# Held operands of the last down phase: own tiles, two transfers, earlier splits

## The chip, the cores and the metric

The kernel runs on one core of a Trainium2 chip. The metric is the device time of one execution in microseconds (us), as the median of several runs. The profile is one execution, taken by the hardware profiler; it names the engines PE (TensorE matmul), PEld (its weight loads), DVE (VectorE), ACT (ScalarE), POOL (GpSimd) and SP (SyncE, which issues nearly all transfers here).

## The reference

The kernel computes one decoder block in float32: attention and pooling heads, then a SwiGLU feed-forward layer, both between RMS norms with scale, shift and gate from a conditioning vector. The change lies in the last line of the feed-forward part:

```python
h = rmsnorm(x, g_ffn_pre[l]) * (1.0 + scale_f) + shift_f
f = (jax.nn.silu(h @ w_gate[l]) * (h @ w_up[l])) @ w_down[l]
x = x + gate_f * rmsnorm(f, g_ffn_post[l])
```

There are 2048 tokens, a model width of 1024 and a feed-forward width of 2816, which is 22 chunks of 128.

## The kernel before

**The number format.** Every float32 operand of a matmul is split in two: a rounded copy on ACT (line 59, the "high" part, type fp32r) and the remainder on DVE (line 60, the "low" part). A product takes three matmuls: high with high, low with high, high with low (lines 69 to 71).

**The down stage.** The tokens are worked on in two halves of 1024 (`sb` 0 and 1). The product with `w_down` is done in Strassen's manner (seven products of quarter matrices for eight): in each half `down` runs seven phases, p1, p2, p6, p7, p5, p4, p3, in that order. A phase has 11 steps (`HF`), one for each chunk of 128 rows of the inner dimension. A step needs a piece `g` of the gated activations and a piece `w` of the weights, 128x512 each; it makes 12 matmuls, three into each of four PSUM banks (`HK` row blocks).

**How a step gets its operands.** `load_g` brings `g` in groups of four chunks (1 MB, two buffers in turn), `load_w` brings `w` one chunk at a time (256 KB, four buffers); both are asked for five steps ahead. `split_gw` splits both, 2 casts on ACT and 2 subtractions on DVE, into pairs from a ring of five and one more (`operand`). The order on PE, ACT, DVE and POOL is the order of the program text; the order of SP's queue is left to the compiler's scheduler. In the loop over steps, for step n first everything registered ahead for n is written out, then the matmuls, then the splits as far as the window of steps holds no more than six pairs (`PAIRS`, two per step: the split of step n+2), then the "takes": the operations that read a finished phase's banks, one or a few steps later.

**The last phase.** In p3 of the second half the last four chunks (7 to 10, `HELD`) are held back: their steps issue no matmuls, and their split pairs go to tiles of their own in the pool `dn1`, not to the ring. After them come four tail steps, one for each row block, that run the 12 held matmuls of that row block, so that the rows are finished one after the other.

**What is around it.** While p3 runs, the takes of p4 finish rows 4 to 7 of the half. For a row i: an addition from PSUM on DVE (line 1363, `y_v`), its square on ACT with the sum (line 1366), a multiply by the gate on POOL (line 1367), the norm (lines 1384 and 1385 on DVE, the power on POOL, line 1386), and the end in two halves: a multiply-add on DVE (line 1394), and a scale on ACT (line 1396) with an addition on POOL (line 1397). Each half is stored by SP (line 1398). The takes of p3, behind the tail steps, do the same for rows 0 to 3 (`y_u`); the very last row's multiply by the gate and both its ends are on DVE. The takes of p5, while p4 runs, add from PSUM, square and multiply by the gate (`c_4` to `c_7`).

Of the kernel before, what the change touches and what calls it, by code (L numbers as in the profile page):

```python
# [9 lines left out]
F32 = mybir.dt.float32  # L10
F32R = mybir.dt.float32r
# [6 lines left out]
P = 128  # L18
# [10 lines left out]
TB = 512  # L29
# [6 lines left out]
PRB = 6  # L36
FT = {"sr": 4, "p1": 1, "u2": 2, "u3": 2, "u4": 1, "cu": 2, "s": 6, "gs": 3, "tr": 4, "gf": 1}
PAIRS, HELD = 6, 4
RB = PAIRS - 1
LOAD_AT = (-20, -8)  # L40
SPLIT_AT = ((-14, -11, -8, -5), (-8, -6, -4, -2))
# [3 lines left out]
def block_kernel(ctx, tc, x, c, w_cond, b_cond, g_mix_pre, g_mix_post, w_in, w_pool,  # L45
                 pool_scale, w_out, g_ffn_pre, g_ffn_post, w_gate, w_up, w_down, out):
    nc = tc.nc
# [6 lines left out]
    def raw(ap):  # L54
        return ap.bitcast(F32)

    def split(hi, lo, src, low=nc.vector):

        nc.scalar.copy(hi, src)  # L59
        low.tensor_tensor(lo, src, raw(hi), ALU.subtract)  # L60
# [12 lines left out]
    def open_pool(stack, name, bufs=1, side=None):  # L73
        kw = {"side": side} if side else {}
        return stack.enter_context(tc.tile_pool(name=name, bufs=bufs, reuse_waits="tile", **kw))
# [4 lines left out]
    def dt(name, shape):  # L80
        return dram.tile(shape, F32, tag=name, name=name)
# [8 lines left out]
    ga = [{n: dt(f"ga{sb}{n}", [P, NF // 2, TB]) for n in ("a11", "a12", "s1", "s2", "s3", "s4", "a22")} for sb in range(2)]  # L90
# [15 lines left out]
    def ft(tag, name, shape=(P, TB)):  # L106
        return fx.tile(list(shape), F32, tag=tag, bufs=FT[tag], name=name)
# [893 lines left out]

    ring = open_pool(ctx, "ring", bufs=RB)
    SBT = S // 2
    NTS = SBT // P
    HF = NF // 2
# [3 lines left out]
    def operand(name):  # L1009
        used[0] += 1  # L1010
        pool = fx if fx is not None and used[0] % (RB + 1) == 0 else ring
        return [pool.tile([P, TB], F32R, tag=f"w{n}", bufs=1 if pool is fx else RB, name=f"{name}_{n}") for n in "hl"]

# [267 lines left out]
    def down(sb, dn):  # L1281
# [12 lines left out]
        def add_block(ps, i, j, g, w):  # L1294
            cols = slice(i * P, (i + 1) * P)
            mm3(ps, [((g[0][:, cols], g[1][:, cols]), w)], first=j == 0, last=j == HF - 1)

        def phase(n, a, b, parts, held=0):

            if b[0] == "b":  # L1300
                src = wd_rows[b[1] == "2"][:, :, (b[2] == "2") * TB:][:, :, 0:TB]
            else:
                src = td[b]
            ph = {}
            QF = 3 if n == "p1" else 4

            def chunk(j):
                name = f"{sb}{n}_{j}"

                def load_g():  # L1310
                    m = min(QF, HF - j)
                    t = (ring, fx)[len(quads) % 2].tile([P, 4, TB], F32, tag="w32", bufs=1, name=f"g{name}")
                    quads.append(t)
                    ph["gq", j // QF] = t
                    nc.sync.dma_start(t[:, 0:m], ga[sb][a][:, j:j + m, :])

                def load_w():
                    ph["w", j] = t = ft("tr", f"w{name}")
                    nc.sync.dma_start(t, src[:, j, :])

                def split_gw():
                    pairs = []
                    for kind, s in (("g", ph["gq", j // QF][:, j % QF, :]), ("w", ph["w", j])):
                        if j >= HF - held:
                            pair = [dn().tile([P, TB], F32R, tag=f"{kind}k{l}", bufs=held, name=f"{kind}{name}{l}") for l in "hl"]
                        else:
                            pair = operand(f"{kind}{name}")
                        split(*pair, s)
                        pairs.append(pair)
                    ph[j] = pairs  # L1330

                def mm():
                    if j == 0:
                        ph["ps"] = [f_ps(f"dn{sb}{n}_{i}") for i in range(HK)]
                    for i in range(HK):
                        add_block(ph["ps"][i], i, j, *ph[j])

                s = Step(2, split_gw, mm)
                if j % QF == 0:
                    s.ahead.append((5, load_g))  # L1340
                s.ahead.append((5, load_w))
                if j == HF - 1:
                    s.take = [(1 + m + (i if n == "p3" and m < 2 else 2 * i), lambda i=i, f=f: f(i, ph["ps"][i]))
                              for i in range(HK) for m, f in enumerate(parts)]
                if held and j >= HF - held:
                    s.mm = lambda: None
                    s.take = []
                return s

            r = [chunk(j) for j in range(HF)]  # L1350
            if held:
                def tail(i):
                    def mm():
                        for j in range(HF - held, HF):
                            add_block(ph["ps"][i], i, j, *ph[j])
                    after = [(i, f) for f in parts[:2]] + ([(i - 1, parts[3])] if i else []) + [(i, parts[2])]
                    after += [(i, parts[3])] * (i == HK - 1)
                    return Step(0, lambda: None, mm, [(1, lambda i=i, f=f: f(i, ph["ps"][i])) for i, f in after])
                r += [tail(i) for i in range(HK)]
            return r  # L1360
# [91 lines left out]
        r = []  # L1452
        for n, a, b, parts in (
                ("p1", "a11", "b11", [p1]),
                ("p2", "a12", "b21", [p2, lambda i, ps: first_half_done(i, ps)]),
                ("p6", "s2", "t2", [p6]),
                ("p7", "s3", "t3", [p7]),
                ("p5", "s1", "t1", [p6, p5, p5_done]),
                ("p4", "a22", "t4", [p4, lambda i, ps: half_done(st["v"][i], HK + i, 0, ps), lambda i, ps: norm(HK + i), p4_end]),
                ("p3", "s4", "b22", [p6, p3_done, lambda i, ps: norm(i), p3_end])):  # L1460
            r += phase(n, a, b, parts, HELD if sb and n == "p3" else 0)
# [117 lines left out]
```

## Time and profile before

| what | value |
|---|---|
| runs | median 2336.19 us of 3 (2331.99 to 2337.07) |
| profiled execution | 2336.15 us |
| its span, first to last instruction | 2334.4 us |
| granted PE clock, mean | 0.99 |
| stretch 2229 to 2281 us: PE, DVE, ACT, POOL busy | 52.00, 30.85, 24.05, 5.18 us |
| 2281 to 2305 us | 24.00, 18.08, 13.32, 8.57 us |
| 2305 to 2326 us | 14.12, 14.74, 6.69, 13.83 us |
| 2326 to 2334 us | 0.00, 4.06, 1.24, 2.37 us |

The profile's lines give a start or a count, durations, the engine, the source line, and the output and input tiles by their names; a bracket names the idle time before the operation and what ended it. In a line of a timeline the first number is the start in us from the start of the span, the second the duration in us. Durations overlap a little (a new operation begins up to 0.08 us before the shown end of the one before). A stretch's line has the busy time of each engine with its count, then the granted clock of PE, the busy share of the DMA engines and their GB/s. In the chain of waits each piece is the work, or "issue" where no work is shown, that the next one waited for. A step of the down stage takes about 2.75 us, and p3 begins near 2285.5 us, p4 near 2255.2, p2 near 2134.

### The profile page before, as it was taken

Reading aid. Unit: us, or ns where it says so; the run is one execution under the profiler, and the core shown is the slowest. Engines: PE = TensorE matmul, PEld = TensorE weight load, DVE = VectorE, ACT = ScalarE, POOL = GpSimd, SP = SyncE. Lnnn points to the kernel's source line nnn. Section 1 sums busy time; section 2 is a strip of 40 time slices with the busy share of each in tenths; the row PEclk is TensorE's granted clock in tenths of the full one; section 3 lists DMA queues with packets and bytes.
Section 4 is the critical chain, followed back from the end, with each engine's and each line's share of the span. In section 5 each row is a group of like instructions: output and inputs, shape, how many; then the busy total and the mean of one; then the engine's idle time right before and its main releaser. Section 6 shows DMA issues by size and latency. Waiting matters only on the chain.

```text
span 2334.4 us, 33386 instructions
## 1 busy us (share of the span) xinstructions
PE 2268.4 (97%) x10717; PEld 1863.7 (80%) x10717; DVE 1633.2 (70%) x2222; ACT 1165.1 (50%) x2411; POOL 1317.9 (56%) x1621
## 2 busy tenths in 40 slices
PE   6999999999999999999999999999999999999997
PEld 4778888888888778787888888788888888888885
DVE  6774559999999966756666665886766555565556
ACT  4323658889988854444323232554533323234444
POOL 4542347787778854555787878430486665641004
PEclk9999999999999999999999999999999999999998
DMA  8785764343435636665545455876753333327664
GB/s 288 250 291 194 275 189 118 100 109 89 129 100 147 174 100 203 212 204 179 168 157 158 156 160 183 267 248 212 249 184 112 109 118 91 113 86 281 194 196 145
DMA packets 307116, 405.17 MB, mean 174 GB/s; under 512 B 19254, under 2 KB 179578, under 8 KB 303868
## 3 DMA queue, kind: packets, MB, share of 16 engines
q1 hardware_dynamic: 302620, 400.68, 53.8%
q10 hardware_dynamic: 4320, 2.36, 0.4%
q8 instruction: 84, 1.38, 0.3%
q14 instruction: 92, 0.75, 0.1%
HBM read 274.51 MB, written 128.45 MB: 173 GB/s over the span
## 4 chain that ended last, share of the span: by engine, by line
PE 81%; DVE 5%; POOL 4%; DMA 4%; issue 3%; ACT 2%; SPq 1%; POOLq 0%; DVEq 0%; ACTq 0%
PE wt L838 4%; PE t_u L71 3%; PE t_u L70 3%; PE t_u L69 3%; PE t_g L70 3%; PE t_g L69 3%; PE t_g L71 3%; PE dn0p L70 3%; PE dn0p L71 3%; PE dn0p L69 3%; PE dn1p L69 3%; PE dn1p L70 3%; PE dn1p L71 3%; PE av L853 3%; PE av L854 2%
## 5 line engine op out<-in xcount | busy, mean ns | idle before, releaser
L827 POOL TENSOR_TENSOR w<-sg,pr 128x512 f32<-128x512 f32 (+2 forms) x320 | 307.8, 962 | 41.6 <-DVE pr L821 22.2
L1186 POOL TENSOR_TENSOR s<-s,cu 128x512 f32<-128x512 f32 x88 | 133.8, 1528 | 239.0 <-DVE cu L1185 138.5
L821 DVE TENSOR_TENSOR_SCAN pr<-pr,carry,idle 128x512 f32<-128x512 f32 x192 | 244.3, 1272 | 0.0
L808 ACT ACTIVATE sg<-z 128x512 f32<-128x512 f32 (+2 forms) x320 | 180.8, 565 | 56.2 <-PE z L806 25.8
L60 DVE TENSOR_TENSOR wtl<-wt,wth 128x512 fp32r<-128x512 f32 (+1 forms) x320 | 189.9, 594 | 26.8 <-ACT wth L59 25.5
L59 ACT CAST wth<-wt 128x512 fp32r<-128x512 f32 (+1 forms) x320 | 179.5, 562 | 12.8 <-PE wt L838 12.8
L810 ACT ACTIVATE pr<-z 128x512 f32<-128x512 f32 (+2 forms) x320 | 179.9, 562 | 0.0
L838 PE MATMUL wt<-ident,w 128*128 128x128 f32 x1088 | 173.7, 274 | 3.7 <-POOL w L827 1.9
L60 DVE TENSOR_TENSOR u_s_l<-u_s,u_s_h 128x512 fp32r<-128x512 f32 x66 | 66.6, 1010 | 151.5 <-ACT u_s_h L59 151.4
L838 PEld LDWEIGHTS wt<-ident,w 128*128 128x128 f32 x1088 | 129.3, 141 | 31.0 <-POOL w L827 2.6
L1176 ACT ACTIVATE s<-s 128x512 f32<-128x512 f32 x88 | 55.7, 633 | 193.3 <-DVE s L1175 193.3
L853 PE MATMUL av<-wth,vt 128*128 128x512 f32 (+1 forms) x320 | 129.2, 404 | 5.9 <-ACT o L858 5.8
L70 PE MATMUL dn0p<-w0p_l,g0p_h 128*128 128x512 f32 x308 | 121.2, 394 | 2.6 <-DVE w0p_l L60 2.6
L60 DVE TENSOR_TENSOR u_a_l<-u,u_a_h 128x512 fp32r<-128x512 f32 x66 | 79.1, 1200 | 61.9 <-ACT u_a_h L59 61.9
L69 PE MATMUL dn0p<-w0p_h,g0p_h 128*128 128x512 f32 x308 | 120.5, 391 | 0.0
L854 PE MATMUL av<-wtl,vt 128*128 128x512 f32 (+1 forms) x320 | 118.8, 371 | 1.7 <-DVE wtl L60 1.3
L71 PE MATMUL dn0p<-w0p_h,g0p_l 128*128 128x512 f32 x308 | 120.4, 391 | 0.0
L803 PE MATMUL z<-kt,qt 128*128 128x512 f32 (+2 forms) x320 | 117.9, 369 | 1.9 <-ACT pr L810 1.3
L59 ACT CAST g_s_h<-g_s 128x512 fp32r<-128x512 f32 x66 | 39.5, 620 | 159.6 <-POOL g_s L1118 83.4
L804 PE MATMUL z<-kt,qt 128*128 128x512 f32 (+2 forms) x320 | 117.0, 366 | 0.0
L59 ACT CAST u_s_h<-u_s 128x512 fp32r<-128x512 f32 x66 | 38.6, 614 | 151.9 <-POOL u_s L1118 151.9
L70 PE MATMUL dn1p<-w1p_l,g1p_h 128*128 128x512 f32 x292 | 114.4, 392 | 0.0
(657 smaller groups left out, 7302.7 us busy)
## 6 DMA issues: line engine op xcount, KB each, us to landing
g<-in_w_gate_dram SPq DMA_DIRECT2D x42, 512.0 KB, 4.7
u<-in_w_up_dram SPq DMA_DIRECT2D x42, 512.0 KB, 4.8
wc<-in_w_cond_dram SPq DMA_DIRECT2D x32, 512.0 KB, 5.8
qt<-qd SPq DMA_DIRECT2D x64, 256.0 KB, 3.9
wd<-in_w_down_dram SPq DMA_DIRECT2D x44, 256.0 KB, 3.0
tdt<-wd SPq DMA_DIRECT2D x44, 256.0 KB, 2.0
w0p<-tdt SPq DMA_DIRECT2D x44, 256.0 KB, 3.4
w1p<-tdt SPq DMA_DIRECT2D x44, 256.0 KB, 2.8
```

The costliest lines, as they stand in the source:

```text
L59: nc.scalar.copy(hi, src)
L60: low.tensor_tensor(lo, src, raw(hi), ALU.subtract)
L69: nc.tensor.matmul(ps, lh, rh, start=first and i == 0, stop=False)
L70: nc.tensor.matmul(ps, lh, rl, start=False, stop=False)
L71: nc.tensor.matmul(ps, ll, rh, start=False, stop=last and i == n - 1)
L808: nc.scalar.activation(sg[:, 0:L], z[:, 0:L], AF.Sigmoid, scale=0.125)
L810: nc.scalar.activation(pr[:, 0:L], z[:, 0:L], AF.Sigmoid, scale=-0.125)
L821: nc.vector.tensor_tensor_scan(pr[:, 0:L][:, ::-1], pr[:, 0:L][:, ::-1], idle[:, 0:L], one if carry is None else carry, ALU.mult, ALU.bypass)
L827: nc.gpsimd.tensor_tensor(w[:, 0:L], sg[:, 0:L], pr[:, 1:L + 1], ALU.mult)
L838: nc.tensor.transpose(wt[:, i * P:(i + 1) * P], wss[u][i][:, b * P:(b + 1) * P], ident)
L853: nc.tensor.matmul(av[:, lo0:], vb, wh[:, lo0:], start=first, stop=False)
L854: nc.tensor.matmul(av[:, lo0:], vb, wl[:, lo0:], start=False, stop=last)
```

## The change

In p3 of the second half the held chunks get functions of their own. `held_load` brings all four `g` pieces in one transfer and all four `w` pieces in another, 1 MB each, into two new tiles in the pool `dn1`; it is asked for 20 steps ahead of p3's first step. `held_chunk` splits chunk 7 at 12 steps ahead of p3's first step, and the next ones two steps later each: at p5's last step and at p4's steps 1, 3 and 5. A held step counts no pairs any more. The ordinary loads leave the held chunks out: four `load_w`, the group of `g` from chunk 8, and one of the four chunks in the group before.

```diff
+HELD_AT = (20, 12)
...
                 def load_g():
-                    m = min(QF, HF - j)
+                    m = min(QF, HF - held - j)
...
-                        if j >= HF - held:
-                            pair = [dn().tile([P, TB], F32R, tag=f"{kind}k{l}", bufs=held, name=f"{kind}{name}{l}") for l in "hl"]
-                        else:
-                            pair = operand(f"{kind}{name}")
+                        pair = operand(f"{kind}{name}")
...
-                if held and j >= HF - held:
-                    s.mm = lambda: None
-                    s.take = []
                 return s
 
-            r = [chunk(j) for j in range(HF)]
+            def held_load():
+                for kind, rows_of in (("g", ga[sb][a]), ("w", src)):
+                    ph[kind] = t = dn().tile([P, held, TB], F32, tag=f"{kind}k", bufs=1, name=f"{kind}k{sb}{n}")
+                    nc.sync.dma_start(t, rows_of[:, HF - held:, :])
+
+            def held_chunk(j):
+
+                def split_gw():
+                    ph[j] = [[dn().tile([P, TB], F32R, tag=f"{kind}k{l}", bufs=held, name=f"{kind}{sb}{n}_{j}{l}") for l in "hl"]
+                             for kind in "gw"]
+                    for kind, pair in zip("gw", ph[j]):
+                        split(*pair, ph[kind][:, j - HF + held, :])
+
+                s = Step(0, lambda: None, lambda: None)
+                m = j - HF + held
+                s.ahead.append((HELD_AT[1] + j - 2 * m, split_gw))
+                if m == 0:
+                    s.ahead.append((HELD_AT[0] + j, held_load))
+                return s
+
+            r = [held_chunk(j) if j >= HF - held else chunk(j) for j in range(HF)]
```

## The prediction

> **What bounds the kernel now.** I read the page first, then the busy time in stretches of the last 30 us, then the timelines of PE, DVE and POOL there, and last the chain of waits. Over the whole span PE is the bound:
>
> ```profile
> span 2334.4 us, 33386 instructions
> PE 2268.4 (97%) x10717; PEld 1863.7 (80%) x10717; DVE 1633.2 (70%) x2222; ACT 1165.1 (50%) x2411; POOL 1317.9 (56%) x1621
> ```
>
> The change touches the down stage of the second half, so the end is what counts. The stretches of the held part (PE busy, granted clock behind the POOL column, DMA share):
>
> ```profile
> 2304.78:2312.40 7.62, 3.77 (x12) 2.01 (x11) 7.28 (x12) 2.36 (x5) 3.89 (x4) 0.82 0.25 93
> 2312.40:2316.60 4.20, 4.20 (x11) 3.23 (x11) 1.67 (x4) 1.45 (x3) 3.26 (x4) 0.51 0.33 125
> ```
>
> In the first, PE is busy for half, DVE nearly throughout; in the second, PE works at half its clock. PE's timeline of that place:
>
> ```profile
> 2304.78 0.39 PE L69 MATMUL dn1p<-w1p_7h,g1p_7h 128*128 128x512 f32 x1
> ...
> 2307.97 0.50 PE L70 MATMUL dn1p<-w1p_9l,g1p_9h 128*128 128x512 f32 x1 [1.09 <-DVE w1p_9l L60]
> ...
> 2309.19 0.50 PE L69 MATMUL dn1p<-w1p_10h,g1p_10h 128*128 128x512 f32 x1 [0.49 <-ACT w1p_10h L59]
> 2311.93 0.80 PE L70 MATMUL dn1p<-w1p_10l,g1p_10h 128*128 128x512 f32 x1 [2.23 <-DVE w1p_10l L60]
> ...
> 2317.37 0.39 PE L69 MATMUL dn1p<-w1p_7h,g1p_7h 128*128 128x512 f32 x1
> ...
> 2322.58 0.39 PE L71 MATMUL dn1p<-w1p_10h,g1p_10l 128*128 128x512 f32 x1
> ```
>
> The tail step of row 0 waits three times, 3.81 us in all, for the split of held chunks 9 and 10. At full clock a matmul starts every (2322.58 - 2317.37) / 23 = 0.227 us, so 48 of them from 2304.78 would end at 2315.7 + 0.2; they end near 2322.8. Of the 7.1 us lost, 3.8 is waiting and 3.3 the lower clock behind it. But PE's end does not set the span's end directly. The chain of waits shows what does:
>
> ```profile
> 2300.13 0.55 POOL fss L1386
> 2300.68 0.80 issue
> 2301.52 1.49 POOL y_v L1397
> 2303.00 1.70 POOL y_v L1367
> 2304.70 1.46 issue
> 2306.19 0.55 POOL fss L1386
> ...
> 2312.21 0.56 POOL fss L1386
> 2312.79 0.75 DVE c_7gs L1394
> 2313.55 0.61 DVE y_u L1363
> ...
> 2316.76 2.30 issue
> 2319.09 1.29 POOL y_u L1367
> ...
> 2330.00 0.75 DVE y_u L1394
> ```
>
> From 2300 on it runs through the finishing of p4's rows on POOL (square's follow-up L1367, the power L1386, the last addition L1397), one row every 6.05 us (2300.13 to 2306.19, then to 2312.21), and only then through p3's four rows. In each turn 1.46 us is "issue": POOL waits for the norm that DVE has not reached. DVE's timeline says why:
>
> ```profile
> 2300.57 0.68 DVE L60 TENSOR_TENSOR g1p_7l<-g1p,g1p_7h 128x512 fp32r<-128x512 f32 x1
> ...
> 2303.48 1.78 DVE L60 TENSOR_TENSOR g1p_8l<-g1p,g1p_8h 128x512 fp32r<-128x512 f32 x1
> ...
> 2311.19 0.68 DVE L60 TENSOR_TENSOR w1p_10l<-w1p,w1p_10h 128x512 fp32r<-128x512 f32 x1
> ...
> 2317.57 0.69 DVE L1363 TENSOR_TENSOR y_u<-dn1p,y_u 128x512 f32<-128x512 f32 x1 [2.28 <-PE dn1p L71]
> ...
> 2320.29 0.69 DVE L1363 TENSOR_TENSOR y_u<-dn1p,y_u 128x512 f32<-128x512 f32 x1 [0.89 <-PE dn1p L71]
> ...
> 2330.67 0.74 DVE L1394 SCALAR_TENSOR_TENSOR c_3gs<-c_3gs,fss,x1b_3cu 128x512 f32<-128x512 f32 x1
> ```
>
> The eight held subtractions (2300.57 to 2311.87) stand between the norms. Where one of them meets a POOL operation, it takes 1.78 us in place of 0.68, and POOL's own operation is stretched too. POOL's unopposed durations are:
>
> ```profile
> 2290.08 1.29 POOL L1367 TENSOR_TENSOR y_v<-y_v,gf 128x512 f32<-128x512 f32 x1 [9.67 <-ACT dn1p L1366]
> 2295.64 1.29 POOL L1397 TENSOR_TENSOR y_v<-y_v,x1b_4cu 128x512 f32<-128x512 f32 x1 [1.81 <-ACT y_v L1396]
> ```
>
> **The change, term by term.** The matmuls, casts and subtractions are the same in number. In the built program's order the only moves on ACT and DVE are four packets of two casts and two subtractions, from p3's steps 5 to 8 to p5's last step and p4's steps 1, 3 and 5. SP loses five issues in p3 (four of w, the quad of chunk 8; chunk 4's quad shrinks by one row block) and gains two. That held steps now count no pairs changes nothing for chunks 0 to 6: their windows of six pairs end where they did.
>
> *First term, p4's rows 6 and 7.* The turn from one power to the next is now 0.80 + 1.49 + 1.70 + 1.46 + 0.55, and 0.05 between. With no held subtraction on DVE, its queue in a turn is a final multiply-add (0.75, row of c_7gs), two norm operations and one addition (0.68): about 1.8 us, less than POOL's own 2.6. So the norm is ready before POOL ends its multiply: the 1.46 goes, and L1397 and L1367 come down to 1.29 each. I leave 0.1 for the norm slipping between them. The turn is 0.80 + 1.29 + 0.10 + 1.29 + 0.55 = 4.03, and two turns save 4.0. Bounds: if the wait goes but POOL stays stretched by DVE's remaining work, the turn is 0.80 + 1.49 + 1.70 + 0.55 = 4.54 and two save 3.0; above 4.0 there is nothing in these rows but the 0.2 for slipping. I take 4.0, because DVE has one large operation per turn left, at the turn's start while POOL still waits for ACT.
>
> *Second term, p3's rows.* The power of row 7 then ends at 2312.77 - 4.0 = 2308.8, the multiply-add of c_7gs at 2309.5, and the first addition of p3, L1363, starts there. PE, without its waits, has row 0 ready at 2304.78 + 12 x 0.227 + 0.2 = 2307.7 and row 1 at 2310.4, while DVE wants row 1 behind the addition and the norm of row 0, near 2311.3. So the 2.28 us wait for PE goes, and with it the 2.30 "issue" in the chain, which is POOL waiting for that row's square. The 0.89 wait for row 2 lies beside a POOL that is busy from 2319.09 to 2322.16, so it is counted at nothing. What is late next is POOL, back to back over its multiplies and additions. Bounds: POOL and DVE now meet once more at c_0's multiply-add, which costs 1.03 if it is stretched as other subtractions were (1.78 against 0.75), so 1.3 below; 2.3 + 0.9 = 3.2 above. I take 2.3.
>
> *The held splits in p4.* They run ahead of a ring split that PE paces. Of one such split the timelines of ACT and DVE show, with the split two steps later:
>
> ```profile
> 2263.51 0.62 ACT L59 CAST g1p_h<-g1p 128x512 fp32r<-128x512 f32 x1 [1.04 <-PE dn1p L70]
> ...
> 2269.02 0.62 ACT L59 CAST g1p_h<-g1p 128x512 fp32r<-128x512 f32 x1 [1.02 <-PE dn1p L70]
> ```
>
> ```profile
> 2264.77 0.68 DVE L60 TENSOR_TENSOR w1p_l<-w1p,w1p_h 128x512 fp32r<-128x512 f32 x1
> ```
>
> A ring split begins when PE frees its pair (2263.51), is done at 2265.45, and is needed two steps later (2269.02): 3.6 us to spare. A held split puts 2 x 0.6 us before it on DVE, up to 1.1 more (1.78 less 0.68) if it meets a POOL multiply, so 2.3 at most, partly in time where ACT idles 1.04 anyway. Behind it on DVE wait the ring split and one addition from PSUM whose banks are not needed until p3. Cost 0; if the cover were gone it would be up to 2.3 for each of four.
>
> *The two transfers.* SP's order was built from the compiler's schedule, and there they stand far earlier than 20 steps ahead of p3: g's behind the last x1b load in phase p2, w's three issues later, ahead of p6's first quad.
>
> The busiest stretch before that place, SP's timeline there, a quad's time to landing, and the cast that wants p6's first quad:
>
> ```profile
> 2125.00:2135.00 10.00, 10.00 (x46) 8.15 (x45) 4.21 (x7) 4.41 (x8) 0.00 (x0) 1.00 1.03 407
> ```
>
> ```profile
> 2141.91 0.43 SPq L1377 DMA_DIRECT2D x1b_3s<-x1d  x1
> 2144.25 3.12 SPq L1319 DMA_DIRECT2D w1p<-in_w_down_dram  x2
> 2149.19 0.33 SPq L1315 DMA_DIRECT2D g1p<-ga1s  x1
> ```
>
> ```profile
> g1p<-ga1s SPq DMA_DIRECT2D x8, 1024.0 KB, 5.0
> ```
>
> ```profile
> 2158.80 0.62 ACT L59 CAST g1p_h<-g1p 128x512 fp32r<-128x512 f32 x1 [1.58 <-PE dn1p L70]
> ```
>
> At the 407 GB/s of a full stretch the 2.1 MB take 5.2 us. If all of it delayed p6's quad (issued 2149.19, 5.0 us to land), that would land at 2159.4, 0.6 us after the cast that wants it (2158.80), and PE still has the 3.6 us above. The two wait for PE instructions of the gate-and-up stage alone, long done. Cost 0, bound 0 from both sides by that spare time. In p3 SP is freed of five loads; the stores behind them are not on the chain.
>
> **Sum.** 4.0 + 2.3 = 6.3 us. The profiled execution took 2336.15 us for its 2334.4 us span (the median of the runs is 2336.19, nearly the same), so 2336.15 - 6.3 = 2329.85. By the bounds, 3.0 + 1.3 = 4.3 gives 2331.9 and 4.2 + 3.2 = 7.4 gives 2328.7.
>
> **Rivals.** 0.2% of the time, 4.7 us, is about what a measurement can tell from no change; the shown runs alone lie 5 us apart.
>
> (a) *POOL and DVE keep blocking each other.* Only the 1.46 waits go, once each and in part (say half, 1.5 in all), and p3 gains 1.3: 2.8 us, 2333.4, no change. For it speaks 1.78 in place of 0.68 wherever the two meet; against it, that in each turn four of the five large DVE operations that POOL can meet are held ones. 0.22. The Trainium skill, "SBUF — State Buffer", section "Who interferes with whom", has this as a rule: a VectorE operation with two SBUF inputs and a GpSimd operation that reads SBUF exclude each other, and the later one waits for the whole of the other; by it the multiply-adds and norms that stay on DVE go on meeting POOL's operations, which then run back to back. The trace agrees that they exclude each other: POOL's 1.29 and one subtraction fit in the 1.78.
>
> (b) *More goes than I count*: with DVE empty, the stretched operations of p3's end (chain from 2319 to 2330) shrink too; two by 1.1 gives 8.5 us and 2327.6. Against it: there DVE and POOL start together on the same power. 0.13.
>
> (c) *Slower: held splits stall PE in p4.* Each of the four delays a ring split; it decides if a ring split is late by more than its 3.6 us to spare. Price 4 x 2.3 plus the lower clock behind each gap (3.3 after 3.8 us of gaps, so 2.0 for each 2.3): 17 us, less 6.3: 2347. Against it: PE never waits in p4 now. 0.06.
>
> (d) *The change doesn't do what it says of the loads*: issued in p2, where DMA was full, they starve PE there for 5.2 us once, and the clock costs 5.2 x 3.3 / 3.8 = 4.5 behind it: 3.4 more than is saved, 2339.5, no change by the bound. Against it: the spare time of p6's quad and of its split. 0.04.
>
> (e) *The half clock stays.* If the slow matmuls near 2312 are not the gaps' doing, PE's row 1 comes 2 us later, 2312.4 in place of 2310.4; DVE would wait 1.1 at row 1, and 5.2 are saved: 2330.95. The clock was 0.51 only behind 3.81 us of gaps, so 0.05. The Trainium skill, "TensorE: Matmul & The Clock Gate", section "Part 1: The HAM clock gate", asks for about 3.4 us of idleness in a window before the clock halves; the longest single gap here is 2.23, so by a strict reading the gaps would be too short.
>
> **How the numbers follow.** My forecast holds 0.50. Faster by over 0.2%: 0.50 + 0.13 + 0.05 = 0.68; within: 0.22 + 0.04 = 0.26; slower: 0.06. The likeliest alone has 2328.7 to 2331.9. To hold eight in ten, the range takes in (b) and (a), with a little for scatter: 2326.5 to 2334.0.
>
> **What would show it.** PE's tail should run 48 matmuls without a wait at clock 1.00 and end near 2316; the powers on POOL for rows 5, 6, 7 should be near 4.0 us apart; L1363 of row 1 should not wait for PE. Held casts should stand in p5 and p4 with no PE wait beside them, and the two transfers should land before 2160. A PE wait between 2150 and 2285, or powers still 6 us apart, would make the prediction wrong.

## The result, and the profile after

The changed kernel took 2329.05 us, median of 13 runs (2326.57 to 2332.79); beside it the kernel before took 2336.95 us, median of 13 (2331.99 to 2341.62). The ratio is 0.9969, with a 95% interval of 0.996 to 0.9977: 0.31% faster, which is 7.2 us (5.4 to 9.3 by the interval). The profiled execution took 2328.57 us for a span of 2326.8 us. The head of its page:

```profile
span 2326.8 us, 33377 instructions
PE 2263.6 (97%) x10717; PEld 1861.9 (80%) x10717; DVE 1630.6 (70%) x2222; ACT 1165.1 (50%) x2411; POOL 1316.5 (57%) x1621
```

The matmuls, casts and subtractions are as many as before. The lines of the code have moved: what was line 69, 1363, 1386 or 1394 is 70, 1378, 1401 or 1409 now.

**A stretch to measure by.** The two spans differ by 7.6 us, but not all of it is the change's doing. The last x1b load (`x1b_3s`, ahead of the first changed instruction) was issued at 2141.91 before and at 2140.86 after; over all profiles of this study it was issued between 2139.4 and 2146.6, with no edit ahead of it. From there to the power of row 4 on POOL it is 151.4 us in either kernel. So the runs are compared below by what is left: from the start of row 4's power to the end of the span. These powers are POOL's timeline of the kernel before (a start, a duration, the operation, and in brackets the idle time before it):

```profile
2293.29 0.55 POOL L1386 TENSOR_TENSOR fss<-fss,mhalf 128x1 f32<-128x1 f32 x1 [1.92 <-DVE fss L1385]
...
2321.59 0.56 POOL L1386 TENSOR_TENSOR fss<-fss,mhalf 128x1 f32<-128x1 f32 x1
...
2325.35 0.55 POOL L1386 TENSOR_TENSOR fss<-fss,mhalf 128x1 f32<-128x1 f32 x1 [0.28 <-DVE fss L1385]
...
2329.41 0.55 POOL L1386 TENSOR_TENSOR fss<-fss,mhalf 128x1 f32<-128x1 f32 x1 [0.28 <-DVE fss L1385]
```

And POOL's timeline of the changed kernel, with one addition between them:

```profile
2292.23 0.55 POOL L1401 TENSOR_TENSOR fss<-fss,mhalf 128x1 f32<-128x1 f32 x1 [1.92 <-DVE fss L1400]
...
2299.08 0.55 POOL L1401 TENSOR_TENSOR fss<-fss,mhalf 128x1 f32<-128x1 f32 x1 [1.49 <-DVE fss L1400]
...
2302.96 0.56 POOL L1401 TENSOR_TENSOR fss<-fss,mhalf 128x1 f32<-128x1 f32 x1
...
2306.86 0.55 POOL L1401 TENSOR_TENSOR fss<-fss,mhalf 128x1 f32<-128x1 f32 x1
...
2312.64 1.74 POOL L1412 TENSOR_TENSOR c_0gs<-c_0gs,x1b_0cu 128x512 f32<-128x512 f32 x1
2314.67 0.55 POOL L1401 TENSOR_TENSOR fss<-fss,mhalf 128x1 f32<-128x1 f32 x1 [0.28 <-DVE fss L1400]
...
2318.47 1.00 POOL L1401 TENSOR_TENSOR fss<-fss,mhalf 128x1 f32<-128x1 f32 x1
...
2321.51 0.55 POOL L1401 TENSOR_TENSOR fss<-fss,mhalf 128x1 f32<-128x1 f32 x1
```

The end stretch was 2334.4 - 2293.29 = 41.11 us and is 2326.8 - 2292.23 = 34.57: 6.54 shorter. Up to row 5's power the two are alike (6.84 and 6.85). From row 5 to row 7 it was 12.08 and is 7.78 (turns of 3.88 and 3.90). Behind row 7's power, row 1's came at +9.38 and comes at +7.81; rows 1 to 2 are alike (3.76 and 3.80); rows 2 to 3 took 4.06 and take 3.04.

The chain of waits of the changed kernel, in order of time:

```profile
2300.46 1.29 POOL y_v L1412
2301.76 0.26 POOL y_v L1382
2302.02 0.94 issue
2302.96 0.56 POOL fss L1401
...
2307.44 0.75 DVE c_7gs L1409
2308.19 0.61 DVE y_u L1378
...
2311.46 1.77 DVE y_u L1409
2313.23 1.18 DVE fss L1399
...
2322.10 0.75 DVE y_u L1409
```

It still runs through POOL and DVE; the "issue" of 2.30 us ahead of row 1 is gone. The 0.94 "issue" in a turn isn't a wait for DVE: POOL's timeline has no bracket at the power of 2302.96, and the multiply (1.31 from 2301.71) fills that time. PE's timeline of the tail steps, and its stretch:

```profile
2303.73 0.39 PE L70 MATMUL dn1p<-w1p_7h,g1p_7h 128*128 128x512 f32 x1
...
2314.43 0.39 PE L72 MATMUL dn1p<-w1p_10h,g1p_10l 128*128 128x512 f32 x1
```

```profile
2304.40:2316.10 11.70, 10.42 (x46) 8.26 (x44) 7.70 (x13) 4.27 (x11) 9.68 (x10) 1.00 0.36 135
```

The 48 tail matmuls start within (2314.43 - 2303.73) / 47 = 0.228 us of each other, at a clock of 1.00 all the way. DVE's timeline shows where the two engines still meet:

```profile
2301.03 0.74 DVE L1399 TENSOR_TENSOR fss<-fss 128x1 f32<-128x1 f32 x1 [0.62 <-ACT dn1p L1381]
...
2309.85 0.68 DVE L1378 TENSOR_TENSOR y_u<-dn1p,y_u 128x512 f32<-128x512 f32 x1
2311.46 1.77 DVE L1409 SCALAR_TENSOR_TENSOR y_u<-y_u,fss,x1b_0s 128x512 f32<-128x512 f32 x1 [0.93 <-POOL fss L1401]
2313.16 1.24 DVE L1399 TENSOR_TENSOR fss<-fss 128x1 f32<-128x1 f32 x1
...
2322.76 0.75 DVE L1409 SCALAR_TENSOR_TENSOR c_3gs<-c_3gs,fss,x1b_3cu 128x512 f32<-128x512 f32 x1
```

Row 1's addition (2309.85) no longer waits for PE. But row 0's multiply-add takes 1.77 in place of the 0.74 that it took before, and row 1's norm 1.24.

Last, the two places to which the work went: SP's timeline in p2 with the stretch behind it, and DVE's timeline in p4:

```profile
2140.86 0.43 SPq L1392 DMA_DIRECT2D x1b_3s<-x1d  x1
2141.39 0.38 SPq L1348 DMA_DIRECT2D gk1p<-ga1s  x1
...
2146.72 0.38 SPq L1348 DMA_DIRECT2D wk1p<-in_w_down_dram  x1
```

```profile
2145.00:2155.00 10.00, 10.00 (x45) 8.21 (x44) 4.84 (x8) 4.56 (x9) 0.00 (x0) 1.00 0.98 367
```

```profile
2262.12 1.23 DVE L61 TENSOR_TENSOR g1p_9l<-gk1p,g1p_9h 128x512 fp32r<-128x512 f32 x1
2263.27 0.68 DVE L61 TENSOR_TENSOR w1p_9l<-wk1p,w1p_9h 128x512 fp32r<-128x512 f32 x1
2263.88 0.68 DVE L61 TENSOR_TENSOR g1p_l<-g1p,g1p_h 128x512 fp32r<-128x512 f32 x1
2264.48 0.68 DVE L61 TENSOR_TENSOR w1p_l<-w1p,w1p_h 128x512 fp32r<-128x512 f32 x1
```

The DMA engines were 0.68 busy in that stretch before and are 0.98 busy now, and PE is busy for all of its 10.00 us in either. In p4 the ring split begins behind a held one: it ends at 2264.48 + 0.68 = 2265.16, which is 2266.21 with the 1.05 us by which the changed kernel runs earlier here, 0.76 later than before (2264.77 + 0.68 = 2265.45). PE waits nowhere from 2090 us to the end.

### The profile page after: what moved, and what is told of

Read it like the earlier page. It is cut to its first block, busy times and chain, and to the rows that moved or that the text cites. A ratio compares the mean times of both kernels' runs of the same rounds, so it can differ in the third digit from the quotient of the medians.

```text
span 2326.8 us, 33377 instructions
## 1 busy us (share of the span) xinstructions
PE 2263.6 (97%) x10717; PEld 1861.9 (80%) x10717; DVE 1630.6 (70%) x2222; ACT 1165.1 (50%) x2411; POOL 1316.5 (57%) x1621
## 4 chain that ended last, share of the span: by engine, by line
PE 82%; DVE 5%; DMA 3%; POOL 3%; issue 3%; ACT 3%; SPq 1%; POOLq 0%; DVEq 0%; ACTq 0%
PE wt L839 4%; PE t_u L71 3%; PE t_u L70 3%; PE t_u L72 3%; PE t_g L71 3%; PE t_g L70 3%; PE t_g L72 3%; PE dn0p L71 3%; PE dn0p L72 3%; PE dn0p L70 3%; PE dn1p L70 3%; PE dn1p L71 3%; PE dn1p L72 3%; PE b_g L71 3%; PE av L854 2%
```

## The experiments

All edits are against the changed kernel. "End stretch" is the one from row 4's power to the end of the span, 34.57 us there and 41.11 before. In the same kernel profiled again it was 34.49, so tenths of it can be read, while the ratios of medians of 5 to 13 runs have intervals some 4 to 6 us wide.

**Loads alone.** The transfers stay early; the splits go back to their old place.

```diff
-                s = Step(0, lambda: None, lambda: None)
+                s = Step(2, split_gw, lambda: None)
...
-                s.ahead.append((HELD_AT[1] + j - 2 * m, split_gw))
```

> Of the change only the tiles and the two early 1-MB transfers are kept; the held splits stand at their old place in p3. My theory: the gain comes from where the splits stand, so the time is that of the kernel before (ratio 0.999 to 1.001), with powers on POOL 6.0 us apart for rows 5 to 7 and 3 to 4 us of PE waits in the tail of row 0. Rival (the loads were late): most of the gain is there, ratio 0.997 to 0.998 and turns near 4 us.

Measured: 2336.34 us, ratio 0.9996 (0.9987 to 1.0005); end stretch 41.42; turns of 6.06 and 6.01. Its waits of PE from 2090 us on (total, times, longest):

```profile
PE dn1p L71 <- DVE w1p_10l L61: 2.2, 1, 2.2
PE dn1p L71 <- DVE w1p_9l L61: 1.1, 1, 1.1
PE dn1p L70 <- ACT w1p_10h L60: 0.5, 1, 0.5
```

They are those of before, with a granted clock of 0.50 in the 4.21 us behind them (2309.89 to 2314.10). So the early loads by themselves give nothing and cost nothing; the gain lies in the place of the splits.

**Subtractions on DVE again.** The operands are ready early, so PE has nothing to wait for, but eight subtractions of the same shape, into spare tiles, stand at the old place.

```diff
+                def again():
+                    for kind, pair in zip("gw", ph[j]):
+                        d = dn().tile([P, TB], F32R, tag=f"{kind}again", bufs=2, name=f"{kind}again{j}")
+                        nc.vector.tensor_tensor(d, ph[kind][:, j - HF + held, :], raw(pair[0]), ALU.subtract)
+
-                s = Step(0, lambda: None, lambda: None)
+                s = Step(2, again, lambda: None)
```

> The changed kernel with eight more subtractions on DVE, of the same operands into tiles nobody reads, at the place where the held ones stood before; PE's operands are early and it need not wait. My theory (DVE's queue is worth 4.0 us, PE's waits 2.3): the turns go back to 5.5 to 6 us, PE has no wait in the tail, and 3.5 to 4.5 us of the gain are lost: about 2333, ratio to before 0.998 to 0.9985. Rival (PE's waits and its lower clock carry the gain): at most 0.5 us lost, ratio 0.997.

Measured: 2335.79 us, ratio 0.9993 (0.9984 to 1.0003); no PE wait; end stretch 38.76. POOL's timeline, and DVE's behind the first line:

```profile
2310.63 0.55 POOL L1406 TENSOR_TENSOR fss<-fss,mhalf 128x1 f32<-128x1 f32 x1 [1.49 <-DVE fss L1405]
...
2316.68 0.55 POOL L1406 TENSOR_TENSOR fss<-fss,mhalf 128x1 f32<-128x1 f32 x1 [1.49 <-DVE fss L1405]
```

```profile
2313.97 1.77 DVE L1361 TENSOR_TENSOR gagain<-gk1p,g1p_10h 128x512 fp32r<-128x512 f32 x1
...
2316.27 0.15 DVE L1404 TENSOR_TENSOR fss<-fss 128x1 f32<-128x1 f32 x1
```

The turns are 6.05 again, with POOL idle for 1.49 before each power, while behind row 7's power nothing changes (15.85 us to the last multiply-add, 15.90 without the subtractions). So the first term is DVE's queue and not PE: it is worth 4.19 of the end stretch. The measured ratio lies above the expected 0.998 to 0.9985, which only the lower end of its interval reaches; the expected loss of 3.5 to 4.5 us is seen in the end stretch. The profiled execution itself issued `x1b_3s` 5.5 us later than that of the changed kernel, so its whole span says nothing of the edit.

**PE late at row 1.** The tail step of row 1 runs chunks 7 to 9 three times, 18 more matmuls; the splits stay early.

```diff
-                        for j in range(HF - held, HF):
+                        for j in [HF - held, HF - held + 1, HF - held + 2] * 2 * (i == 1) + list(range(HF - held, HF)):
```

> The changed kernel, where PE multiplies chunks 7 to 9 of row 1 into its bank three times in place of once: 18 more matmuls, 4.1 us, ahead of row 1's end, and that row's result is another. My theory (a wait of DVE for PE at row 1 goes into the end nearly in full, as the 2.28 us did before the change): DVE waits 3.4 to 3.8 us at row 1 and the tail grows by 2 to 3.5 us, to 36.6 to 38.1 us. Rival (PE's end has time to spare and the whole gain is DVE's queue): DVE waits, but the tail grows by less than 0.7 us.

Measured: 2336.31 us in one run; turns of 3.88 and 3.91; end stretch 38.25, 3.68 longer, a little above the 2 to 3.5 expected. DVE's timeline:

```profile
2317.51 0.69 DVE L1378 TENSOR_TENSOR y_u<-dn1p,y_u 128x512 f32<-128x512 f32 x1 [3.56 <-PE dn1p L72]
```

DVE takes up row 1 at 6.63 us behind row 7's power (2310.88) here, 5.36 before and 2.99 after; from that power to the last multiply-add it is 19.72, 18.46 and 15.90. So 2.37 us of lateness cost 2.56 before, and 3.64 cost 3.82 here, where PE has no wait and its clock is 1.00: PE's lateness at row 1 is paid in full, whether waits or more matmuls make it late. The turn of the last row goes back to 4.07 too (3.04 in the changed kernel, 4.06 before). The second term, in both its pieces, is PE's lateness, apart from the first.

**All four held splits at one step** (p4's third), to see how much room p4 has.

```diff
-                s.ahead.append((HELD_AT[1] + j - 2 * m, split_gw))
+                s.ahead.append((8 + j, split_gw))
```

> All four held splits at one step, p4's step 3, in place of four steps. My theory (a ring split has 3.6 us to spare): eight subtractions, 4.9 us and 0.6 for a meeting with POOL, come before one ring split, which ends 0.8 us after PE wants it; one PE wait of 0.4 to 1.2 us near 2268, none else, and the time is 0.4 to 1.2 us above the changed kernel's, ratio to before 0.997 to 0.9975. Rival (less to spare, and a gap lowers the clock): several PE waits, 3 us or more lost, ratio 0.998 or above.

Measured: 2331.92 us, ratio 0.9977 (0.9966 to 0.9988); end stretch 34.58. PE's timeline has one wait, and DVE's shows the subtraction that it waits for:

```profile
2269.85 0.50 PE L71 MATMUL dn1p<-w1p_l,g1p_h 128*128 128x512 f32 x1 [0.48 <-DVE w1p_l L61]
```

```profile
2269.12 0.68 DVE L61 TENSOR_TENSOR w1p_l<-w1p,w1p_h 128x512 fp32r<-128x512 f32 x1
```

The way from `x1b_3s` to row 4's power is 152.13 us in place of 151.37: 0.76 lost, inside the 0.4 to 1.2; the medians, 2.9 us apart, can't show it. This profile issued `x1b_3s` when the kernel before did (2141.89 and 2141.91), so their times can be set side by side: with eight subtractions ahead of it the ring split ends at 2269.80, where it ended at 2265.45 before. It is 4.35 later, and PE waits for 0.48 of that. So some 3.9 us were to spare, near the 3.6 predicted, and a held split by itself makes the ring split only 0.76 later.

**Eight transfers of 256 KB in place of two of 1 MB.**

```diff
-                    nc.sync.dma_start(t, rows_of[:, HF - held:, :])
+                    for l in range(held):
+                        nc.sync.dma_start(t[:, l, :], rows_of[:, HF - held + l, :])
```

> The changed kernel with the held operands brought by eight transfers of 256 KB in place of two of 1 MB. My theory (the loads are hidden either way): time and tail as the changed kernel's, ratio to before 0.9965 to 0.9975, tail 34.4 to 34.8 us. Rival (the size of the transfers matters): PE or ACT wait for them, or ring loads come late, and 1 us or more is lost.

Measured: 2329.18 us, ratio 0.9962 (0.9948 to 0.9975); end stretch 34.49; no PE wait. The size of the transfers doesn't matter.

**Ends on DVE.** Both halves of every row's end are multiply-adds on DVE; ACT and POOL lose theirs.

```diff
-                if half or sb and row == HK - 1:
+                if half or sb:
```

> The changed kernel, and in the second half both ends of every row are a multiply-add on DVE, in place of ACT's scale and POOL's addition for one of them. My theory (POOL, back to back, bounds the end, and DVE is half idle): a turn falls from 3.9 to about 3.5 us, since POOL's multiply and DVE's two multiply-adds exclude each other, and the end comes 2.5 us sooner (1.5 to 4): ratio to before 0.995 to 0.9965. Rival (DVE is the next bound): no gain or up to 2 us lost, ratio 0.997 to 0.998.

Measured: 2328.89 us, ratio 0.9963 (0.9951 to 0.9976); end stretch 33.59, 0.98 shorter. The turns are 3.43 and 3.43, as expected, so POOL's addition did set the 3.9. But rows 7 to 0 take 4.69 (4.02 in the changed kernel), and the last row takes 3.66 (3.04): DVE, now with two multiply-adds a row, gives 0.67 and 0.62 back there, 1.3 of the 2.3 that the other rows and the end save. The size (1.5 to 4) was missed for that; the ratio lies in its range, but can't tell such sizes apart.

**The norm with a scalar operand.** The first norm operation takes the second sum as a scalar operand, not as a second tensor.

```diff
-            nc.vector.tensor_tensor(r, r, st["ss"][:, row, 1:2], ALU.add)
-            nc.vector.tensor_scalar(r, r, 1.0 / D, EPS, ALU.mult, ALU.add)
+            if sb:
+                nc.vector.tensor_scalar(r, r, st["ss"][:, row, 1:2], 1.0 / D, ALU.add, ALU.mult)
+                nc.vector.tensor_scalar(r, r, 1.0, EPS, ALU.mult, ALU.add)
+            else:
+                nc.vector.tensor_tensor(r, r, st["ss"][:, row, 1:2], ALU.add)
+                nc.vector.tensor_scalar(r, r, 1.0 / D, EPS, ALU.mult, ALU.add)
```

> The changed kernel, with the norm's first operation on DVE (second half only) as a tensor-scalar form: one row of sums as the tensor, the other as the scalar, in place of a two-tensor addition. The tail is read as the time from row 4's power on POOL to the end of the span: 41.11 us before the change, 34.57 after. My theory (an operation with two SBUF inputs on DVE and one on POOL exclude each other, others don't): the norm never takes more than 0.2 us (now 0.74 to 1.24 where it meets POOL), and the tail shortens by 0.5 to 1.2 us, ratio to before 0.996 to 0.997. Rival (any DVE operation is held up by POOL): the norm stays at 0.7 to 1.2 us there and the tail at 34.6.

Measured: 2331.32 us, ratio 0.9974 (0.9963 to 0.9985); end stretch 34.05, 0.52 shorter, at the low edge; the ratio lies above the expected 0.996 to 0.997. DVE's timeline:

```profile
2304.45 0.21 DVE L1400 TENSOR_SCALAR fss<-fss 128x1 f32<-128x1 f32 x1 [0.61 <-ACT dn1p L1381]
...
2314.88 1.80 DVE L1413 SCALAR_TENSOR_TENSOR y_u<-y_u,fss,x1b_0s 128x512 f32<-128x512 f32 x1 [0.89 <-POOL fss L1405]
2316.60 0.20 DVE L1400 TENSOR_SCALAR fss<-fss 128x1 f32<-128x1 f32 x1
```

The norm's first operation is never held up (0.20 to 0.21, where it took 0.74 and 1.24). The multiply-add of row 0, which still reads two tensors, still is (1.80). The turns in p4 stay at 3.89: there the norm was hidden behind POOL's multiply.

**Both together, spread.** The scalar norm; the ends of rows 0, 2, 3 and 4 alone on DVE; p4's takes at steps 0, 1, 3 and 4 (0, 2, 4 and 6 in the changed kernel), so that rows 4 to 7 are done sooner.

```diff
-                if half or sb and row == HK - 1:
+                if half or sb and row in (0, 2, 3, 4):
...
-                s.take = [(1 + m + (i if n == "p3" and m < 2 else 2 * i), lambda i=i, f=f: f(i, ph["ps"][i]))
+                s.take = [(1 + m + (i if n == "p3" and m < 2 else (0, 1, 3, 4)[i] if n == "p4" and sb else 2 * i), lambda i=i, f=f: f(i, ph["ps"][i]))
```

> The changed kernel with the norm of one input, both ends on DVE for rows 0, 2 and 4 too, and p4's rows taken up at p3's steps 0, 1, 3 and 4 in place of 0, 2, 4 and 6. My theory (the tail is bound by operations of DVE and POOL that exclude each other, and p3's steps have room for more of them since the held splits left): rows 4 to 7 are done by about 2304, PE waits nowhere, and the tail is 2 to 3.3 us shorter than the changed kernel's, 31.3 to 32.6 us, ratio to before 0.9945 to 0.9965. Rival (DVE is full in p3's steps, and ring splits come late): PE waits in p3, and the gain is under 1 us or lost.

Measured: 2330.63 us, ratio 0.9968 (0.9955 to 0.998); no PE wait; end stretch 32.03, 2.54 shorter. DVE's timeline now waits for PE again, at each of p3's rows:

```profile
2314.09 0.69 DVE L1378 TENSOR_TENSOR y_u<-dn1p,y_u 128x512 f32<-128x512 f32 x1 [0.84 <-PE dn1p L72]
...
2319.53 0.69 DVE L1378 TENSOR_TENSOR y_u<-dn1p,y_u 128x512 f32<-128x512 f32 x1 [0.63 <-PE dn1p L72]
```

So PE now paces p3's rows; how much more could be gained behind it was not tried. Row 7's power starts 12.68 us behind row 4's (14.63 in the changed kernel), so 1.95 of the 2.54 are gained in p4's rows. Three things were changed at once, and no run here separates their shares. The ratio lies above the expected 0.9945 to 0.9965. As the median didn't show the 2.5 us, this version and the changed kernel were run again side by side:

> The changed kernel itself again, on the same chip and in the same rounds as the spread version, so that their medians can be set against each other. Theory: 0.9972 of before, give or take 0.001; the stretch from row 4's power to the end of the span 34.6 us (34.3 to 34.9) as in the first profile, and the turns between the powers 3.9 us. Rival (the first profile's end was a lucky one): the stretch over 35.5 us.

> The spread version (norm with a scalar operand, the ends of rows 0, 2, 3 and 4 on DVE, p4's takes at steps 0, 1, 3 and 4) again, beside the changed kernel on one chip. Theory: its stretch from row 4's power to the end of the span is 32.0 us (31.7 to 32.4), 2.5 us shorter than the changed kernel's, and since nothing earlier is slowed its median is 1.5 to 3.5 us under that of the changed kernel. Rival: the earlier takes cost in p4 what the end saves; then the medians lie within 1 us of each other though the end is 2.5 us shorter.

Measured beside 2338.11 us for the kernel before: the changed kernel 2330.79 us, ratio 0.9967 (0.9956 to 0.9979), end stretch 34.49; the spread version 2326.21 us, ratio 0.9951 (0.9937 to 0.9964), end stretch 2330.1 - 2298.08 = 32.02. From `x1b_3s` to row 4's power it is 151.4 and 151.5, so the earlier takes cost nothing ahead of it. The end is 2.5 us shorter in both profiles. The medians were 4.6 us apart here, more than the 3.5 expected; over both series they are 2330.15 us (19 runs) and 2329.72 us (10 runs), and the ratios' intervals overlap. That the version beats the kernel before is shown; that it beats the changed kernel is shown by its end alone, not yet by its time.

## Why the prediction was right

**The sum.** 6.3 us were predicted and 6.54 measured in the end stretch: 4.30 and 2.56 for the two terms, less 0.31 behind the last multiply-add (3.73 us from its start to the end of the span before, 4.04 after). The other 1.05 us between the spans arose ahead of the first changed instruction. That the median, 2329.05 us, came within 0.8 of the forecast 2329.85 is in part luck: the interval of the gain, 5.4 to 9.3 us, is wider than that.

**First term**, 4.0 predicted, 4.30 measured. The turn came out at 3.88 and 3.90 for 4.03, so that the term lies 0.1 above its upper bound of 4.2: the sum of durations, 0.80 + 1.29 + 1.29 + 0.55, counts the overlaps (the addition of 1.29 at 2300.46 is followed at 2301.71). The 0.1 allowed for the norm wasn't needed: the norm does get held up, to 0.74, but it ends while POOL's multiply is still running, so that this follows the addition at once and the power follows the multiply at once. The subtractions put back on DVE, with PE free of waits, bring the 6.05 back: that this term is DVE's queue is shown.

**Second term**, 2.3 predicted, 2.56 measured, but it came in two pieces, and only one was where the prediction had it. The wait for PE at row 1 went, and with it POOL's idle time there (2.33 in POOL's timeline). DVE's and POOL's timelines of the kernel before show how the two operations that are stretched now stood there:

```profile
2318.18 0.74 DVE L1394 SCALAR_TENSOR_TENSOR y_u<-y_u,fss,x1b_0s 128x512 f32<-128x512 f32 x1
```

```profile
2320.34 1.30 POOL L1397 TENSOR_TENSOR c_0gs<-c_0gs,x1b_0cu 128x512 f32<-128x512 f32 x1
```

Of the 2.33, POOL lost 0.44 again as c_0's addition came to 1.74 for 1.30, and 0.28 to waiting for row 1's norm, which stood behind the stretched multiply-add of row 0: 1.6 net, near the lower bound of 1.3. The bound had the mechanism right (POOL and DVE meet once more there) and named the wrong operation, c_0's multiply-add; c_0's end is an addition on POOL, and the one that DVE was held at is row 0's. The other 1.0 came at the last row, which was counted at nothing. There the timelines of POOL and DVE show of the kernel before:

```profile
2327.31 1.82 POOL L1397 TENSOR_TENSOR c_2gs<-c_2gs,x1b_2cu 128x512 f32<-128x512 f32 x1 [1.41 <-ACT c_2gs L1396]
```

```profile
2327.93 1.22 DVE L1384 TENSOR_TENSOR fss<-fss 128x1 f32<-128x1 f32 x1
```

c_2's addition was stretched by row 2's multiply-add, and row 3's norm was held up beside it; in the changed kernel the norm is done before that addition starts:

```profile
2320.17 0.15 DVE L1399 TENSOR_TENSOR fss<-fss 128x1 f32<-128x1 f32 x1
```

```profile
2320.30 1.26 POOL L1412 TENSOR_TENSOR c_2gs<-c_2gs,x1b_2cu 128x512 f32<-128x512 f32 x1 [0.83 <-ACT c_2gs L1411]
```

This is what rival (b) spoke of, at 1.0 and not its 2.2. The two errors, 0.7 too much and 1.0 too little, nearly cancel, and that is luck.

**The clock.** The half clock went with the gaps, and it came back with them in the run with the loads alone (0.50): rival (e) falls. The Trainium skill, "TensorE: Matmul & The Clock Gate", section "Part 1: The HAM clock gate", has the clock halve after an idle window of some 3.4 us; in two profiles it halved behind gaps of 1.09, 0.49 and 2.23 us with matmuls between them, none of them so long, so here the measurement decides. By the starts of the matmuls PE lost the 7.1 us of the prediction (the 48th at 2322.58 in place of 2315.45); its two ends, 2315.9 and 2322.8, are 6.9 apart, since the 0.2 was added to one alone.

**Held splits at no cost.** Right, and the price was over-estimated: the two held subtractions that met POOL's multiplies took 1.23 and 1.22, so 0.55 more and not 1.1. The one at 2262.12 began 0.62 us into the multiply of c_4 (POOL, 2261.50) and had only its rest to wait for. Rival (c) falls, as PE never waits in p4. Its mechanism appears only with all four splits at one step, and there once, at 0.76 us with the clock at 1.00, where (c) had 4.3 for each of four.

**Loads at no cost.** Right: they were issued where the built order had them, the DMA engines filled up to 0.98, and PE didn't wait. The transfer of g landed 7.6 us after its issue, near 2149; the trace has no landing for that of w. Rival (d) falls by the run with the loads alone.

**Rival (a)** falls with the turns of 3.9. The two engines go on meeting, but in the turns of rows 6 and 7 the one operation of DVE that is held up, the norm, fits beside POOL's own 2.6 us of a turn. That they exclude each other was argued from a wrong sum: 1.29 and a subtraction of 0.68 make 1.97 and don't fit in 1.78. What an operation waits for is the rest of the one that is running, as the 1.23 above shows.

## What to carry to other kernels

Where two in-order engines hand a row to and fro, other work in either queue lengthens every turn, though neither engine is the bound of the whole kernel: it stands ahead of the hand-over, and it holds up the other engine where they meet. Eight subtractions cost 4.2 us so, by the run that put them back. Move it to a stage that another engine paces, and take the spare time there from the timeline of the work that comes behind it. When a change is worth a few microseconds of thousands, find two fixed instructions around it and compare that stretch: what lay ahead of the change here varied by up to 7.2 us from run to run, as much as the change was worth.

## What the runs showed of the hardware

The norm's first operation, on 128x1 elements, takes 0.15 us, and 0.74 to 1.24 us where it meets a POOL operation; with a scalar operand in place of the second tensor it takes 0.21 beside POOL as well. The additions of a PSUM bank and one tile (0.67 to 0.69) weren't held up either, while multiply-adds and subtractions of two tiles were (1.77 for 0.74, 1.23 and 1.78 for 0.68). The Trainium skill, "SBUF — State Buffer", section "Who interferes with whom", has it so: a VectorE operation with two SBUF inputs contends with a GpSimd one that reads SBUF, and one with at most one SBUF input, outside the modes that use both ports, does not. The traces agree for all the operations just named.

The early stages, the same in all these kernels, reached the last x1b load at times up to 7.2 us apart. What sets that isn't known from these runs.
